# Values in one stationary operand: two products for three in a gated hybrid block

## The chip, the core and the metric

The kernel runs on one core of a Trainium2 chip. The metric is the device time of one execution in microseconds, the median over several. Five engines work side by side, each with its own queue in order: TensorE (PE, with its weight loads shown as PEld), VectorE (DVE), ScalarE (ACT), GpSimd (POOL) and SyncE (SP), which here only issues DMAs. The products go to eight banks, of 512 float32 per partition each, and ScalarE and VectorE take them from there.

## What is computed

One layer of a hybrid encoder on x of 512 positions by 1024 channels, in float32. The parts that matter here:

```
h    = rms_norm(x, g)
proj = h @ w_in          # conv B, C, in | q | k | v | forget logits | gates
F    = cumsum(log_sigmoid(f + b_f))
s    = q.k / sqrt(64) + F[t] - F[s],  s <= t
o    = softmax(s) v      # 8 heads of 64
x    = x + (sigmoid(gA) * y_conv + sigmoid(gB) * (o @ w_out_attn)) @ w_o
x    = x + w_down(silu(a) * b),  [a|b] = dwconv3(rms_norm(x) @ w_up)
out  = rms_norm(x)
```

## The kernel before

**Arithmetic.** A float32 operand is split into two parts of the type float32r: `hi`, the rounded copy (made by ScalarE), and `lo`, what is left of it (a subtraction by VectorE). A product is then three matmuls, hi by hi, lo by hi and hi by lo, which `mm3` (L240) issues one after another into the same bank. The product of the two lo parts is left out.

**Layout.** Channels or positions lie on 128 partitions. x is held as eight blocks `xs` of 128 channels by 512 positions; `xgh` and `xgl` (L384, L393) are the two parts of x times the norm's scale, which stands in `vec`, a tile with all scales and small weights as columns. Weights come in as a stream of chunks of 128 x 1024 (`raw`), and `split` (L196 to L227) makes `wh` and `wl` of each, with two buffers for each part, so that the next chunk is split while the one in use is multiplied.

**Order of the program.** (1) v and the forget logits for all positions, from eight chunks `v0` to `v7`, kb by kb (L378 to L426), while x arrives; nine calls on a tile of ones (18 PE instructions, `warm`, L101) stand ahead of them on TensorE. (2) `evac_v` (L629) scales v and splits it into `vh` and `vl`. (3) q and k of the first two pairs of heads. (4) The attention loop (L681): 32 units of (pair, head e of the pair, block qb of 128 queries). Unit i issues its two score matmuls, then one half of a projection from the list `fill` (24 matmuls, for the convolution, q, k and gates), then the transposes `tp` of unit i - 3 into one of two banks (5 and 6, in turn), and after every second query block of head 1 `attend` (L575), five units behind the scores. (5) The gates, mix, w_o, and the channel mixer, none of which the change touches.

**attend.** For a pair of heads and half of the queries (256), o of shape 128 x 256 is collected in bank 7: the first 64 partitions are head 0 and the others head 1. The stationary operand holds 64 columns of v and 64 columns of zeros, in this order for head 0 and the other way round for head 1. To this end `vh` and `vl` have three slots of 64 with zeros in the middle (two GpSimd memsets, L340). For each head and each block kb of keys three matmuls: `vh` by `pth`, `vl` by `pth`, `vh` by `ptl`, where `pth` and `ptl` are the two parts of the transposed probabilities. The last kb covers only 128 of the 256 queries. The halves have 2 and 4 blocks of keys, so an attend has 12 or 24 matmuls. Then ScalarE copies o to `oth` (L589) and VectorE makes `otl` (L590), which `ya` (L729 to L733) reads in the mix.

**The start.** L353 to L366 write out the order of the first transfers. SP's queue: first half of xs block 0, second part of chunk v0, second half of block 0, block 1, v1, block 2, v2, and so on. ScalarE's queue: first part of v0, then 40 columns of `vec` (the scales). The first `xgh` piece (L384) waits for the half of block 0 and for these columns. The rest of `vec` follows later (L366).

**What sets the order.** `keep` fixes TensorE's matmuls, the DMAs and the start in program order; ScalarE's and VectorE's other instructions are put in order by the scheduler.

Of the kernel before, what the change touches and what calls it, by code (L numbers as in the profile page):

```python
# [8 lines left out]
F32 = mybir.dt.float32  # L9
F32R = mybir.dt.float32r  # L10
AF = mybir.ActivationFunctionType
ALU = mybir.AluOpType

P = 128
D = 1024
S = 512
KB = D // P
NT = S // P
H = 8
HD = 64  # L20
# [11 lines left out]
PADL, PADR = 16, 120  # L32


G1, G2, GF, BG, CM, CF, BF = 0, 8, 16, 24, 40, 52, 184
ME, MO = 185, 186
NV = 187
VW = 4 * HD + H
PADW = {"h": 32, "l": 16}

# [17 lines left out]
def block_kernel(ctx, tc, xT, vecs, wv, win, wmix, wo, wup, wst, wdp, outT):  # L58
# [3 lines left out]
    nc = tc.nc  # L62
# [6 lines left out]
    def keep(ins):  # L69
        return tc.keep_in_program_order(ins)  # L70
# [13 lines left out]

    vec = cp.tile([P, NV], F32, tag="vec", name="vec")

    def col(i):
        return vec[:, i : i + 1]
# [221 lines left out]
    xgh = abp.tile([P, KB, S], F32R, tag="xgh", name="xgh")  # L310
    xgl = abp.tile([P, KB, S], F32R, tag="xgl", name="xgl")
    oth = abp.tile([P, 4, S], F32R, tag="oth", name="oth")
    otl = abp.tile([P, 4, S], F32R, tag="otl", name="otl")
# [20 lines left out]
    )  # L334


    vh = ap.tile([P, NT, 4, 3, HD], F32R, tag="vh", name="vh")
    vl = ap.tile([P, NT, 4, 3, HD], F32R, tag="vl", name="vl")
    for t in (vh, vl):
        nc.gpsimd.memset(t.bitcast(F32)[:, :, :, 1, :], 0.0)  # L340

    ssq = ct("ssq1")
    pa = [bank(t, f"pa{t}") for t in range(NT)]
# [4 lines left out]
    def load_x(kb, cs=slice(0, S)):  # L348
        if kb == len(xs):
            if kb % 2 == 0:  # L350
                load_x.t = ap.tile([P, 2, S], F32, tag="qt" if kb < 4 else "ka", name=f"xs{kb}", bufs=2)
            xs.append(load_x.t[:, kb % 2, :])
        keep(nc.sync.dma_start(xs[kb][:, cs], xT[:, kb, cs]))  # L353


    halves = [slice(0, S // 2), slice(S // 2, S)]
    load_x(0, halves[0])
    load(0)
    keep(nc.scalar.dma_start(vec[:, :CM], vecs[:, :CM]))
    load_x(0, halves[1])  # L360
    for kb in range(1, AHEAD + 1):
        load_x(kb)
# [2 lines left out]
        load_x(kb)  # L365
    keep(nc.sync.dma_start(vec[:, CM:], vecs[:, CM:]))  # L366

    def square_x(kb):
        if kb == 0:
            keep(nc.scalar.activation(ssq, xs[kb], AF.Square))  # L370
            return
        sq = ap.tile([P, S], F32, tag="pp", name=f"sq{kb}", bufs=NPP)
        keep(nc.scalar.activation(sq, xs[kb], AF.Square))
        keep(nc.vector.tensor_add(ssq, ssq, sq))
# [1 line left out]

    squares = ((), (0,), (1,), (2, 3), (4, 5), (6,), (7,), ())
    for kb in range(KB):  # L378
        x = xs[kb]
        cuts = halves if kb == 0 else [slice(0, S)]  # L380

        def x_hi():
            for cs in cuts:
                keep(nc.scalar.activation(xgh[:, kb, cs], x[:, cs], AF.Copy, scale=col(G1 + kb)))  # L384


        if kb == 1:
            x_hi()
        wh, wl = chunk(f"v{kb}")
        if kb != 1:  # L390
            x_hi()
        for cs in cuts:
            keep(nc.vector.scalar_tensor_tensor(  # L393
                xgl[:, kb, cs], x[:, cs], col(G1 + kb), xgh.bitcast(F32)[:, kb, cs],
                op0=ALU.mult, op1=ALU.subtract,
            ))
        for i in squares[kb]:
            square_x(i)

        def vmm(t, x, w, start, stop, parts=(0, 1)):  # L400
            xt = x[:, kb, t * P : (t + 1) * P]
            if 0 in parts:
                keep(nc.tensor.matmul(pa[t][:, :VW], xt, w[:, :VW], start=start, stop=stop))
            if 1 in parts:
                keep(nc.tensor.matmul(
                    pb[t], xt, w[:, VW:], start=start and t % 2 == 0, stop=stop and t % 2 == 1
                ))

        trio = ((xgh, wh), (xgh, wl), (xgl, wh))
        if kb == 0:  # L410

            for i, (x, w) in enumerate(trio):
                for t0 in (0, 2):
                    for part in (0, 1):
                        for t in (t0, t0 + 1):
                            vmm(t, x, w, i == 0, False, (part,))
        elif kb < KB - 1:
            for x, w in trio:
                for t in range(NT):
                    vmm(t, x, w, False, False)  # L420
        else:
            for t in range(NT):
                for i, (x, w) in enumerate(trio):
                    vmm(t, x, w, False, i == 2)
                if t == 0:
                    rc1 = rstd_col([ssq], NT, 6, "n1")  # L426
# [148 lines left out]
    def attend(pr, half):  # L575
        o = bank(7, f"o{pr}{half}")
        nk = 2 * half + 2
        for e in range(2):
            th, tl = PT.pop((pr, e, half))
            for kb in range(nk):  # L580
                cs = slice(P, 2 * P) if kb == nk - 1 else slice(0, 2 * P)
                wh = vh[:, kb, pr, e : e + 2, :].rearrange("p a b -> p (a b)")
                wl = vl[:, kb, pr, e : e + 2, :].rearrange("p a b -> p (a b)")
                mm3(
                    o[:, cs], wh, wl, th[:, kb, cs], tl[:, kb, cs],
                    e == 0 and kb == 0, e == 1 and kb == nk - 1,
                )
        hs = slice(half * 2 * P, (half + 1) * 2 * P)
        nc.scalar.activation(oth[:, pr, hs], o[:, : 2 * P], AF.Copy)  # L589
        nc.vector.tensor_sub(otl[:, pr, hs], o[:, : 2 * P], oth.bitcast(F32)[:, pr, hs])  # L590


    def run_all(fs):
# [35 lines left out]
    def evac_v(g, t):  # L629
        p = (pa, pb)[g][t]  # L630
        src = p[:, : 4 * HD].rearrange("p (a b c) -> p a b c", a=2, b=2)
        pr = slice(2 * g, 2 * g + 2)
        for e in range(2):
            nc.scalar.activation(vh[:, t, pr, 2 * e, :], src[:, :, e, :], AF.Copy, scale=rc1[:, t : t + 1])
            nc.vector.scalar_tensor_tensor(
                vl[:, t, pr, 2 * e, :], src[:, :, e, :], rc1[:, t : t + 1],
                vh.bitcast(F32)[:, t, pr, 2 * e, :], op0=ALU.mult, op1=ALU.subtract,
            )


# [446 lines left out]
def _layout(i):  # L1087

    import numpy as np

    i = {k: np.asarray(v) for k, v in i.items()}
    f = np.float32

    def cols(v):
        return v.reshape(-1, P).T

    def taps(w):
        return w.reshape(3, -1, P).transpose(2, 1, 0)

    def blocks(w):  # L1100

        k, n = w.shape
        return w.reshape(k // P, P, n // P, P).transpose(2, 1, 0, 3).reshape(n // P, P, k)

    x = i["x"][0]
    wi = i["w_in"][0]
    vecs = np.zeros((P, NV), f)
    vecs[:, G1 : G1 + 8] = cols(i["norm_mix_g"][0])
    vecs[:, G2 : G2 + 8] = cols(i["norm_ffn_g"][0])
    vecs[:, GF : GF + 8] = cols(i["norm_f_g"])  # L1110
    vecs[:, BG : BG + 16] = cols(i["b_gate"][0])
    vecs[:, CM : CM + 12] = taps(i["conv_mix_w"][0]).reshape(P, 12)
    cf = taps(i["conv_ffn_w"][0])
    cf = np.stack([cf[:, :NP], cf[:, NP:]], axis=2)
    vecs[:, CF : CF + 132] = cf.reshape(P, 132)
    for g, (me, mo) in enumerate(((1, 0), (0, 1), (-1, 0), (0, -1))):
        vecs[g * H : (g + 1) * H, BF] = i["b_f"][0]
        vecs[g * H : (g + 1) * H, ME] = me
        vecs[g * H : (g + 1) * H, MO] = mo

    wqk = wi[:, 3 * CW : 3 * CW + 2 * S]
    wvv = wi[:, 3 * CW + 2 * S : 3 * CW + 3 * S]
    o = 3 * CW + 3 * S
    wf = wi[:, o : o + H]
    win = np.concatenate([blocks(wi[:, : 3 * CW]), blocks(wqk), blocks(wi[:, o + H :])])
    wv = np.concatenate([wvv[:, : 4 * HD], wf, wvv[:, 4 * HD :]], axis=1).reshape(KB, P, S + H)
    wmix = np.concatenate([i["w_out_conv"][0], i["w_out_attn"][0]], axis=0)
    wup = blocks(i["w_up"][0])
    wup = np.stack([wup[:NP], wup[NP:]], axis=1).reshape(2 * NP, P, D)
    wdn = blocks(i["w_down"][0]).reshape(KB, P, NP, P)  # L1130
    wst = []
    for d in STEPS[0] + STEPS[1]:
        def pick(*which):
            return [wdn[2 * i + m, :, 2 * q + k] for i, q in d for m, k in which]

        w = pick((1, 1), (0, 0), (0, 1)) + pick((1, 0), (1, 0)) + pick((1, 1), (0, 0))
        wst.append(np.concatenate(w, axis=1))
    wst = np.stack(wst)
    wdp = np.concatenate([wdn[m, :, k] for m, k in PLAIN], axis=1)
    return {  # L1140
        "xT": x.T.reshape(KB, P, S).transpose(1, 0, 2),
        "vecs": vecs,
        "wv": wv,
        "win": win,
        "wmix": blocks(wmix),
        "wo": blocks(i["w_o"][0]),
        "wup": wup,
        "wst": wst,
        "wdp": wdp,
    }  # L1150
# [24 lines left out]
```

## Time and profile before

| | |
|---|---|
| median of 3 timed runs, us | 718.02 (717.55 to 1015.26) |
| span of the profiled execution, us | 716.9 |
| mean granted TensorE clock | 0.997 |
| DMA | 78.07 MB, mean 109 GB/s |
| first attend starts | 82.97 us |
| last attend ends | 188.87 us |
| ACT copy of o to oth | x8, 0.38 us each |
| DVE subtraction for otl | x8, 0.42 us each |

The page gives the span, from the first to the last instruction; the timed runs hold what lies around it too. A row of the timeline has start and duration in us, engine, line, operation, output and inputs, shape, count, and in brackets the idle time before it with what ended it. A row of groups ends in busy us, mean ns of one, and idle us before them. Matmuls overlap, so a row's duration is longer than the distance to the next row; the distance is the cost.

### The profile page before, as it was taken

Reading aid. Unit: us, or ns where it says so; the run is one execution under the profiler, and the core shown is the slowest. Engines: PE = TensorE matmul, PEld = TensorE weight load, DVE = VectorE, ACT = ScalarE, POOL = GpSimd, SP = SyncE. Lnnn points to the kernel's source line nnn. Section 1 sums busy time; section 2 is a strip of 40 time slices with the busy share of each in tenths; the row PEclk is TensorE's granted clock in tenths of the full one; section 3 lists DMA queues with packets and bytes.
Section 4 is the critical chain, followed back from the end, with each engine's and each line's share of the span. In section 5 each row is a group of like instructions: output and inputs, shape, how many; then the busy total and the mean of one; then the engine's idle time right before and its main releaser. Section 6 shows DMA issues by size and latency. Waiting matters only on the chain. (4 is left out here: it accounts for less than half of the span.)

```text
span 716.9 us, 14589 instructions
## 1 busy us (share of the span) xinstructions
PE 705.7 (98%) x6129; PEld 703.3 (98%) x6129; DVE 472.3 (66%) x711; ACT 317.6 (44%) x494; POOL 170.0 (24%) x188
## 2 busy tenths in 40 slices
PE   9999999999999999999999999999999999999996
PEld 9999999999999999999999999999999999999995
DVE  6677767665444444454458777789894677878963
ACT  6665545544433333333345434445433344444542
POOL 5124434222000000123311011045640111116202
PEclk9999999999999999999999999999999999999998
DMA  7513122122123333443314333357863233246313
GB/s 246 172 62 118 62 62 87 60 72 77 60 89 110 98 92 107 156 130 123 103 59 119 91 99 106 97 131 172 202 166 119 89 100 107 89 130 154 93 31 118
DMA packets 28113, 78.07 MB, mean 109 GB/s; under 512 B 3440, under 2 KB 6128, under 8 KB 28048
## 3 DMA queue, kind: packets, MB, share of 16 engines
q1 hardware_dynamic: 23296, 69.32, 31.5%
q0 software_dynamic: 3344, 6.59, 4.8%
q10 hardware_dynamic: 1408, 1.24, 0.5%
q8 instruction: 48, 0.79, 0.4%
q14 instruction: 17, 0.14, 0.1%
HBM read 74.97 MB, written 2.10 MB: 108 GB/s over the span
## 5 line engine op out<-in xcount | busy, mean ns | idle before, releaser
L248 PE MATMUL p_up<-x1l,wh_up 128*128 128x256 f32 x536 | 104.4, 276 | 0.0
L248 PE MATMUL p_up<-x1h,wl_up 128*128 128x256 f32 x536 | 104.4, 276 | 0.0
L248 PE MATMUL p_up<-x1h,wh_up 128*128 128x256 f32 x536 | 104.4, 276 | 0.0
L216 ACT ACTIVATE wh_up<-raw_up 128x1024 fp32r<-128x1024 f32 x44 | 46.7, 1060 | 89.1 <-PE p_up L248 68.8
L248 PEld LDWEIGHTS p_up<-x1l,wh_up 128*128 128x128 f32 x536 | 80.7, 188 | 0.0
L248 PEld LDWEIGHTS p_up<-x1h,wl_up 128*128 128x128 f32 x536 | 80.7, 188 | 0.0
L248 PEld LDWEIGHTS p_up<-x1h,wh_up 128*128 128x128 f32 x536 | 80.6, 188 | 0.0
L220 DVE TENSOR_TENSOR wl_in<-raw_in,wh_in 128x1024 fp32r<-128x1024 f32 x36 | 50.7, 1409 | 30.1 <-ACT wh_in L216 29.6
L220 DVE TENSOR_TENSOR wl_up<-raw_up,wh_up 128x1024 fp32r<-128x1024 f32 x44 | 53.8, 1223 | 20.6 <-ACT wh_up L216 20.6
L248 PE MATMUL p_in<-xgh,wh_in 128*128 128x256 f32 x288 | 56.9, 279 | 1.0 <-ACT wh_in L216 1.0
L216 ACT ACTIVATE wh_in<-raw_in 128x1024 fp32r<-128x1024 f32 x36 | 38.1, 1059 | 42.6 <-PE ya L248 12.7
L248 PE MATMUL p_in<-xgl,wh_in 128*128 128x256 f32 x288 | 56.5, 277 | 0.0
L248 PE MATMUL p_in<-xgh,wl_in 128*128 128x256 f32 x288 | 56.4, 277 | 0.0
L825 DVE TENSOR_TENSOR fz<-p_up,rb_n 128x512 f32<-128x512 f32 x44 | 30.3, 690 | 30.1 <-PE p_up L248 30.0
L838 POOL TENSOR_TENSOR ge<-fu,fu 128x512 f32<-128x512 f32 x11 | 17.1, 1551 | 126.1 <-DVE fu L498 113.3
L248 PEld LDWEIGHTS p_in<-xgh,wh_in 128*128 128x128 f32 x288 | 44.7, 188 | 1.9 <-ACT wh_in L216 1.2
L248 PEld LDWEIGHTS p_in<-xgl,wh_in 128*128 128x128 f32 x288 | 43.6, 188 | 0.0
L248 PEld LDWEIGHTS p_in<-xgh,wl_in 128*128 128x128 f32 x288 | 43.5, 188 | 0.0
L266 PE MATMUL p_up<-x1h,wh_up 128*128 128x256 f32 x168 | 40.3, 277 | 0.0
L266 PE MATMUL p_up<-x1l,wh_up 128*128 128x256 f32 x168 | 40.2, 276 | 0.0
L737 POOL TENSOR_TENSOR g<-g,g 128x512 f32<-128x512 f32 x8 | 10.3, 1292 | 121.3 <-DVE g L736 121.3
L495 DVE SCALAR_TENSOR_TENSOR fu<-fz,vec,fu 128x511 f32<-128x511 f32 x44 | 34.2, 780 | 1.5 <-ACT fu L494 1.5
(268 smaller groups left out, 2021.4 us busy)
## 6 DMA issues: line engine op xcount, KB each, us to landing
raw_up<-in_wup_dram SPq DMA_DIRECT2D x44, 512.0 KB, 3.4
raw_in<-in_win_dram SPq DMA_DIRECT2D x36, 512.0 KB, 3.5
raw_P<-in_wst_dram SPq DMA_DIRECT2D x17, 384.0 KB, 4.1
raw_F<-in_wst_dram SPq DMA_DIRECT2D x17, 256.0 KB
raw_F<-in_wst_dram POOLq DMA_DIRECT2D x17, 256.0 KB, 4.9
raw_mix<-in_wmix_dram SPq DMA_DIRECT2D x8, 512.0 KB, 3.6
raw_wo<-in_wo_dram SPq DMA_DIRECT2D x8, 512.0 KB, 6.3
xr<-in_xT_dram POOLq DMA_DIRECT2D x8, 256.0 KB, 4.9
```

The costliest lines, as they stand in the source:

```text
L216: ins = nc.scalar.activation(hi, raw, AF.Copy)
L220: ins = nc.vector.tensor_sub(lo, raw, hi.bitcast(F32))
L248: keep(nc.tensor.matmul(out[:, cs], w, x[:, cs], start=start and i == 0 and c == 0, stop=stop and i == 2 and c == len(cut) - 1,))
L266: keep(nc.tensor.matmul(out, wl if x == 1 else wh, xl if x == 2 else xh, start=opens and bk not in seen, stop=closes and bk not in left,))
L495: nc.vector.scalar_tensor_tensor(u[:, 1:], z[:, : S - 1], col(w + 1), u[:, 1:], op0=ALU.mult, op1=ALU.add)
L737: nc.gpsimd.tensor_add(a, a, b)
L825: nc.vector.tensor_mul(z, p, rb2)
L838: keep(nc.gpsimd.tensor_mul(ge, a.rearrange(halves_of, h=2), b.rearrange(halves_of, h=2)))
```

## The change

**Values.** One tile `vv` replaces `vh` and `vl`: for each block of positions and each head 128 columns, hi and lo side by side; hi in the head's own half (columns 0 to 63 for head 0, 64 to 127 for head 1), lo in the other. `evac_v` writes it with the same instructions as before. `attend` issues two matmuls in place of three, `vv` by `pth` and `vv` by `ptl`. Head 0 collects in the first 256 columns of bank 7, head 1 in the other 256. In each, the own half of the partitions holds the hi products and the other half the lo products (the lo by lo product among them). So they have to be added across partitions: ScalarE copies the other half into the own partitions of a new tile `os` (64 x 256), VectorE adds the own half, for each head; then oth and otl are made of `os`. The two memsets go.

**Start.** The first half of x's block 0 is laid on the host into `vecs`, between the scales and the rest. One DMA of 296 columns, first on SP's queue, brings both; ScalarE's queue loses its second DMA, SP's the one of the half block. The instructions that read this half read `vec`. The square of block 0 becomes two instructions of 256 columns.

```diff
+XV = 40
+NV = 187 + 256
...
-    vh = ap.tile([P, NT, 4, 3, HD], F32R, tag="vh", name="vh")
-    vl = ap.tile([P, NT, 4, 3, HD], F32R, tag="vl", name="vl")
-    for t in (vh, vl):
-        nc.gpsimd.memset(t.bitcast(F32)[:, :, :, 1, :], 0.0)
+    vv = ap.tile([P, NT, 4, 2, P], F32R, tag="vv", name="vv")
...
-    load_x(0, halves[0])
+    keep(nc.sync.dma_start(vec[:, :CM], vecs[:, :CM]))
     load(0)
-    keep(nc.scalar.dma_start(vec[:, :CM], vecs[:, :CM]))
     load_x(0, halves[1])
...
+    def x_of(kb, cs):
+        return vec[:, XV : XV + S // 2] if kb == 0 and cs.start == 0 and cs.stop == S // 2 else xs[kb][:, cs]
...
-            keep(nc.scalar.activation(ssq, xs[kb], AF.Square))
+            for h in halves:
+                keep(nc.scalar.activation(ssq[:, h], x_of(0, h), AF.Square))
...
-                wh = vh[:, kb, pr, e : e + 2, :].rearrange("p a b -> p (a b)")
-                wl = vl[:, kb, pr, e : e + 2, :].rearrange("p a b -> p (a b)")
-                mm3(
-                    o[:, cs], wh, wl, th[:, kb, cs], tl[:, kb, cs],
-                    e == 0 and kb == 0, e == 1 and kb == nk - 1,
-                )
+                os_ = slice(e * 2 * P + cs.start, e * 2 * P + cs.stop)
+                for i, x in enumerate((th, tl)):
+                    keep(nc.tensor.matmul(
+                        o[:, os_], vv[:, kb, pr, e, :], x[:, kb, cs],
+                        start=e == 0 and kb == 0 and i == 0, stop=e == 1 and kb == nk - 1 and i == 1,
+                    ))
...
-        nc.scalar.activation(oth[:, pr, hs], o[:, : 2 * P], AF.Copy)
-        nc.vector.tensor_sub(otl[:, pr, hs], o[:, : 2 * P], oth.bitcast(F32)[:, pr, hs])
+        w = ap.tile([P, 2 * P], F32, tag="os", name=f"os{pr}{half}", bufs=2)
+        for e in range(2):
+            own, other = (slice(x * HD, (x + 1) * HD) for x in (e, 1 - e))
+            oe = o[:, e * 2 * P : (e + 1) * 2 * P]
+            nc.scalar.activation(w[own, :], oe[other, :], AF.Copy)
+            nc.vector.tensor_add(w[own, :], oe[own, :], w[own, :])
+        nc.scalar.activation(oth[:, pr, hs], w, AF.Copy)
+        nc.vector.tensor_sub(otl[:, pr, hs], w, oth.bitcast(F32)[:, pr, hs])
...
+            own, other = (slice(x * HD, (x + 1) * HD) for x in (e, 1 - e))
-            nc.scalar.activation(vh[:, t, pr, 2 * e, :], src[:, :, e, :], AF.Copy, scale=rc1[:, t : t + 1])
+            nc.scalar.activation(vv[:, t, pr, e, own], src[:, :, e, :], AF.Copy, scale=rc1[:, t : t + 1])
...
+    vecs[:, XV : XV + S // 2] = x.T[:P, : S // 2]
```

How this stands in the queues. TensorE at the first attend (pair 0, first half), from its start to the first product of head 1; before:

```order
L248 MATMUL o_1176<-pth_942,vh 128x256
L248 MATMUL o_1176<-pth_942,vl 128x256
L248 MATMUL o_1176<-ptl_943,vh 128x256
L248 MATMUL o_1176<-pth_942,vh 128x128
L248 MATMUL o_1176<-pth_942,vl 128x128
L248 MATMUL o_1176<-ptl_943,vh 128x128
L248 MATMUL o_1176<-pth_982,vh 128x256 [waits Activation_49]
```

and after:

```order
L584 MATMUL o_1173<-pth_939,vv 128x256
L584 MATMUL o_1173<-ptl_940,vv 128x256
L584 MATMUL o_1173<-pth_939,vv 128x128
L584 MATMUL o_1173<-ptl_940,vv 128x128
L584 MATMUL o_1173<-pth_979,vv 128x256 [waits Activation_49]
```

Four products in place of six for a head, two of each width; the wait for the probabilities of head 1 stays.

ScalarE behind this attend (`pth` copies transposed probabilities out, `pp` is the exponential of the next scores, `wh_in` the hi part of the next weights); before:

```order
L572 ACTIVATE pth_1168<-tp_1170 128x3x128 [waits PE_49]
L589 ACTIVATE oth<-o_1176 128x256 [waits PE_49]
L549 ACTIVATE pp_1196,m_1194<-s_1191,m_1194 128x128 [waits DVE_49]
L216 ACTIVATE wh_in_1226<-raw_in_929 128x1024 [waits DMAHW6_49,PE_49,Activation_49]
L572 ACTIVATE pth_1126<-tp_1241 128x4x128 [waits PE_49]
```

and after:

```order
L572 ACTIVATE pth_1165<-tp_1167 128x3x128 [waits PE_49]
L593 ACTIVATE os_1182<-o_1173 64x256 [waits PE_49]
L549 ACTIVATE pp_1194,m_1192<-s_1189,m_1192 128x128 [waits DVE_49]
L593 ACTIVATE os_1182<-o_1173 64x256 [waits DVE_49]
L595 ACTIVATE oth<-os_1182 128x256 [waits DVE_49]
L217 ACTIVATE wh_in_1224<-raw_in_926 128x1024 [waits DMAHW5_49,PE_49,Activation_49]
L572 ACTIVATE pth_1123<-tp_1239 128x4x128 [waits PE_49]
```

Two instructions more, and the two that now stand ahead of wh_in wait for VectorE.

SP's queue at the start; before:

```order
L353 DMA xs_115<-in_xT_dram 128x256
L153 DMA raw_v_117<-in_wv_dram 128x256
L353 DMA xs_115<-in_xT_dram 128x256
L353 DMA xs_115<-in_xT_dram 128x512
L157 DMA raw_v_123<-in_wv_dram 128x520
```

and after:

```order
L355 DMA vec<-in_vecs_dram 128x296
L154 DMA raw_v_113<-in_wv_dram 128x256
L351 DMA xs_116<-in_xT_dram 128x256
L351 DMA xs_116<-in_xT_dram 128x512
L158 DMA raw_v_119<-in_wv_dram 128x520
```

Only the first transfer differs, in its source and by 40 columns.

More of the change, by code (lines that the diff above doesn't have):

```diff
@@ L32 @@
 PADL, PADR = 16, 120
-G1, G2, GF, BG, CM, CF, BF = 0, 8, 16, 24, 40, 52, 184
-ME, MO = 185, 186
-NV = 187
+G1, G2, GF, BG, CM, CF, BF = 0, 8, 16, 24, 296, 308, 440
+ME, MO = 441, 442
+XV = 40
+NV = 187 + 256
 VW = 4 * HD + H
@@ L378, in block_kernel @@
     for kb in range(KB):
-        x = xs[kb]
         cuts = halves if kb == 0 else [slice(0, S)]
@@ L383, in x_hi @@
             for cs in cuts:
-                keep(nc.scalar.activation(xgh[:, kb, cs], x[:, cs], AF.Copy, scale=col(G1 + kb)))
+                keep(nc.scalar.activation(xgh[:, kb, cs], x_of(kb, cs), AF.Copy, scale=col(G1 + kb)))
         if kb == 1:
@@ L393, in block_kernel @@
             keep(nc.vector.scalar_tensor_tensor(
-                xgl[:, kb, cs], x[:, cs], col(G1 + kb), xgh.bitcast(F32)[:, kb, cs],
+                xgl[:, kb, cs], x_of(kb, cs), col(G1 + kb), xgh.bitcast(F32)[:, kb, cs],
                 op0=ALU.mult, op1=ALU.subtract,
@@ L633, in evac_v @@
         for e in range(2):
-            nc.scalar.activation(vh[:, t, pr, 2 * e, :], src[:, :, e, :], AF.Copy, scale=rc1[:, t : t + 1])
+            own, other = (slice(x * HD, (x + 1) * HD) for x in (e, 1 - e))
+            nc.scalar.activation(vv[:, t, pr, e, own], src[:, :, e, :], AF.Copy, scale=rc1[:, t : t + 1])
             nc.vector.scalar_tensor_tensor(
-                vl[:, t, pr, 2 * e, :], src[:, :, e, :], rc1[:, t : t + 1],
-                vh.bitcast(F32)[:, t, pr, 2 * e, :], op0=ALU.mult, op1=ALU.subtract,
+                vv[:, t, pr, e, other], src[:, :, e, :], rc1[:, t : t + 1],
+                vv.bitcast(F32)[:, t, pr, e, own], op0=ALU.mult, op1=ALU.subtract,
             )
```

## The prediction

> **What bounds the kernel now.** I read the page's busy times first, then the list of waits for TensorE alone, then the stage that the change touches.
>
> ```profile
> span 716.9 us, 14589 instructions
> PE 705.7 (98%) x6129; PEld 703.3 (98%) x6129; DVE 472.3 (66%) x711; ACT 317.6 (44%) x494; POOL 170.0 (24%) x188
> ```
>
> TensorE is busy for 705.7 of 716.9 us, and the next engine, VectorE, for 66%. The waits of TensorE leave nothing in the attention stage:
>
> ```profile
> PE dn L266 <- DVE wl_F L220: 1.2, 3, 0.5
> PE p_in L248 <- ACT wh_in L216: 1.0, 1, 1.0
> ```
>
> The columns are total us, times, longest. These two rows are the longest with products of the kernel in them; dn belongs to the mixer behind attention, and the wait on wh_in comes once, ahead of the first transposes. From the first attend to the last, the stretch reads so (busy us and count of PE, PEld, DVE, ACT, POOL, then clock, DMA share, GB/s):
>
> ```profile
> 84.40:186.10 101.70, 101.70 (x872) 101.19 (x871) 63.34 (x144) 46.56 (x104) 28.75 (x41) 1.00 0.23 71
> ```
>
> TensorE is busy for all 101.70 us at the full granted clock, ScalarE for 46%, VectorE for 62%. So here time is the number of matmuls times their spacing. A matmul taken out shortens the span by its spacing, as long as no wait takes its place.
>
> **The matmuls removed.** These are the products that write o, and the two instructions that take o out:
>
> ```profile
> L248 PE MATMUL o<-pth,vh x48: 220/276/369, 83.0 to 188.6; 128*128 128x256 f32 x32, 128*128 128x128 f32 x16
> L248 PE MATMUL o<-pth,vl x48: 273/276/283, 83.2 to 188.6; 128*128 128x256 f32 x32, 128*128 128x128 f32 x16
> L248 PE MATMUL o<-ptl,vh x48: 274/276/286, 83.3 to 188.8; 128*128 128x256 f32 x32, 128*128 128x128 f32 x16
> L589 ACT ACTIVATE oth<-o x8: 372/383/384, 84.6 to 189.1; 128x256 fp32r<-128x256 f32 x8
> L590 DVE TENSOR_TENSOR otl<-o,oth x8: 415/419/420, 85.7 to 189.7; 128x256 fp32r<-128x256 f32 x8
> ```
>
> There are 144, in 8 attends; 96 stay, so 48 go: 32 with 256 moving columns and 16 with 128. The 276 ns are a latency, since they overlap. The cost is the distance from start to start (first column, us), in the first attend and at the two ends of the last:
>
> ```profile
> 82.97 0.37 PE L248 MATMUL o<-pth,vh 128*128 128x256 f32 x1
> 83.17 0.28 PE L248 MATMUL o<-pth,vl 128*128 128x256 f32 x1
> 83.29 0.28 PE L248 MATMUL o<-ptl,vh 128*128 128x256 f32 x1
> 83.40 0.22 PE L248 MATMUL o<-pth,vh 128*128 128x128 f32 x1
> 83.46 0.28 PE L248 MATMUL o<-pth,vl 128*128 128x128 f32 x1
> 83.57 0.27 PE L248 MATMUL o<-ptl,vh 128*128 128x128 f32 x1
> 83.69 0.33 PE L248 MATMUL o<-pth,vh 128*128 128x256 f32 x1
> ...
> 84.37 0.33 PE L540 MATMUL s<-a_k,a_q 128*128 128x256 f32 x1
> ...
> 186.15 0.28 PE L248 MATMUL o<-pth,vh 128*128 128x256 f32 x1
> ...
> 188.87 0.33 PE L248 MATMUL yc<-ych,wh_mix 128*128 128x256 f32 x1
> ```
>
> An attend of the first half takes 84.37 - 82.97 = 1.40 us for 12 matmuls, one of the second half 188.87 - 186.15 = 2.72 us for 24. Four of each make 4 x (1.40 + 2.72) = 16.5 us for 144, or 0.114 us each. The removed one is the middle of each trio; in the rows it takes 0.12 at 256 columns (83.17 to 83.29) and 0.11 at 128 (83.46 to 83.57), so the mean holds for it: 48 x 0.114 = **5.5 us saved**. Bounds: if a 128-column product in a pair were worth only the 0.06 that the first of a trio shows (83.40 to 83.46), it is 32 x 0.114 + 16 x 0.06 = 4.6; at most it is 48 x 0.12 = 5.8. I take 5.5, because in a pair the second 128-column product still follows the first as the middle one does now.
>
> The Trainium skill (TensorE: Matmul & The Clock Gate, section Back-to-back issue gap) gives N/2.4 + 2.5 ns for a matmul on its own, some 109 ns at 256 columns and 56 at 128. The trace agrees at 256 (0.11 to 0.12) and for the first of a 128-column trio (0.06), not for its second and third (0.11, 0.12). By that rule alone the estimate would be 32 x 0.109 + 16 x 0.056 = 4.4 us saved.
>
> **The evacuation added.** Per attend there were one ScalarE copy (0.38) and one VectorE subtraction (0.42), in series. Now there are three of each, strictly in turn: two halves of 64 partitions on each engine, then the old two on the sum. Does half the partitions halve the time? A row with 64 partitions beside one with 128:
>
> ```profile
> L482 ACT ACTIVATE a_q<-t_q 64x512 fp32r<-64x512 f32 x8 | 5.0, 631 | 3.9 <-DVE t_q L471 3.8
> L572 ACT ACTIVATE pth<-tp 128x512 fp32r<-128x512 f32 x8 | 4.7, 586 | 2.1 <-PE tp L569 2.0
> ```
>
> No: 64x512 takes 631 ns on ScalarE, 128x512 586. VectorE's pair of 64x512 further down takes 1.71, or 0.86 each. So a 64x256 piece costs 0.38 on ScalarE (the row of oth) and 0.42 on VectorE (that of otl, and half of 0.86). Per attend that is 2 x 0.38 + 2 x 0.42 = 1.6 us of chain; in all ScalarE gains 6.1 us and VectorE 6.7, which in the 96.7 us that are left of that stretch makes 54% and 72%. No engine becomes the bound.
>
> The chain can cost only through its queue: ScalarE's second os copy waits for VectorE, and the copies of tp and wh_in stand behind it. Who is late then? The transposes alternate between two banks, so the one at 94.30 needs the bank of the one at 87.44, which VectorE leaves last:
>
> ```profile
> 87.44 0.60 PE L569 MATMUL tp<-ident,pp 128*128 128x128 f32 x4
> 90.88 0.60 PE L569 MATMUL tp<-ident,pp 128*128 128x128 f32 x4
> 94.30 0.27 PE L569 MATMUL tp<-ident,pp 128*128 128x128 f32 x1
> ```
>
> ```profile
> 86.35 0.16 DVE L552 RECIPROCAL m<-m 128x1 f32<-128x1 f32 x1 [0.25 <-ACT pp L549]
> 88.32 0.43 DVE L545 CUSTOM_DVE_ANT_0 s<-s,strip 128x256 f32<-128x256 f32 x1 [1.81 <-PE s L541]
> ...
> 90.53 0.68 DVE L573 TENSOR_TENSOR ptl<-tp,pth 128x512 fp32r<-128x512 f32 x1
> ...
> 91.31 1.71 DVE L484 TENSOR_TENSOR kb<-t_k,a_k 64x512 fp32r<-64x512 f32 x2
> ```
>
> That copy ends at 91.21, 3.1 us before it is needed. The 1.6 us fit in, and VectorE sat idle for 1.81 us just where the new additions come. I cost the chain at 0; without this cover it is 1.6 us eight times, 12.8. Bounds 0 and 12.8; I take 0 because of the 3.1.
>
> After the last attend nobody hides it but yc: ya starts at 191.66 and reads the last quarter of oth and otl at 193.70, 4.8 us after o was done at 188.87.
>
> ```profile
> 191.66 0.39 PE L248 MATMUL ya<-oth,wh_mix 128*128 128x256 f32 x2
> ...
> 193.70 0.39 PE L248 MATMUL ya<-oth,wh_mix 128*128 128x256 f32 x2
> ```
>
> The chain is 3 x 0.38 + 3 x 0.42 = 2.4 us and some hand-overs. Cost 0.
>
> **The start.** One DMA less on ScalarE's queue, the same bytes; the scales now come with the first half of x, first on SP's queue and ahead of the same transfers as before.
>
> ```profile
> 1.05 4.21 PE L101 MATMUL warm<-ones 128*128 128x128 f32 x18 [1.05 <-DVE ones L93]
> 4.94 0.81 PE L403 MATMUL pa<-wh_v,xgh 128*128 128x264 f32 x2
> ...
> 8.62 0.28 PE L403 MATMUL pa<-wh_v,xgh 128*128 128x264 f32 x1
> ```
>
> ```profile
> 4.38 0.91 ACT L384 ACTIVATE xgh<-xs,vec 128x256 fp32r<-128x256 f32 x2 [2.15 <-DMA vec<-in_vecs_dram]
> 7.02 0.72 ACT L384 ACTIVATE xgh<-xs,vec 128x512 fp32r<-128x512 f32 x1 [1.74 <-DMA xs<-in_xT_dram]
> 7.81 0.64 ACT L216 ACTIVATE wh_v<-raw_v 128x520 fp32r<-128x520 f32 x1
> ```
>
> ```profile
> 0.73 0.37 SPq L353 DMA_DIRECT2D xs<-in_xT_dram  x1
> ```
>
> ```profile
> 0.00:4.94 4.94, 3.89 (x19) 3.89 (x19) 1.43 (x4) 2.05 (x4) 4.26 (x13) 1.00 0.59 135
> xs<-in_xT_dram SPq DMA_DIRECT2D x2, 128.0 KB, 2.8
> ```
>
> ScalarE waited 2.15 us for the scales. From its issue at 0.73 the first half of x takes 2.8 us, plus 20 KB at 135 GB/s, 0.15: the first xgh could begin at 3.7 instead of 4.38. But TensorE fills 1.05 to 4.94 with 18 warm products without a gap (3.89 us busy), and the first real one starts as they end, 0.1 after its xgh. So nothing is gained before 4.94. Then kb=1 starts at 8.62, after wh_v at 7.81 + 0.64 = 8.45, which follows the whole x block awaited until 7.02: a later landing would be lost one for one. The bytes ahead of it are the same; bounds -0.1 and +0.15, I take 0. The square of the first block becomes two pieces of at most 0.38 each, behind the wh_v that TensorE awaits, and two GpSimd memsets go, on an engine busy for 24%. Both 0.
>
> **Sum.** -5.5 + 0 + 0: the span goes from 716.9 to 711.4. The median run took 718.02 and the fastest 717.55, so 0.7 to 1.1 us lie around the span; I keep that distance and take 5.5 from the median 718.02: **712.5 us**. With the bounds of the removed products and of the start, and the 0.5 us between runs, the forecast's own range is 712.0 to 713.8.
>
> **The rivals.**
> 1. The hand-over blocks ScalarE (slower). Place: its second os copy, with the copy of tp and wh_in behind it. If each of VectorE's two additions stands behind a pair like the 1.71 one, the delay is 2 x 1.71 + 1.6 = 5.0 us; over the 3.1 that is 1.9 per attend, 15 in all, and 718.0 - 5.5 + 15 = 727.7. It decides from 3.1 us of delay and turns the balance at 3.1 + 0.7 = 3.8. For it: the order gives that second copy a wait on VectorE. Against: VectorE's idle 1.81 us there. A milder form, 0.2 to 0.5 us stalled per attend, gives back 1.5 to 4: 714 to 716.5.
> 2. The start gains as well: if TensorE could begin when xgh is ready, 0.7 us earlier, 711.8. For: the 2.15 us wait. Against: warm products run up to 4.94.
> 3. The pairs pay the smaller price, 4.6 saved, 713.4. For it: the 0.06 of a trio's first product. Against: the 0.11 and 0.12 of the others. By the rule of the Trainium skill above it would be 713.6.
> 4. The two products do not run at the spacing of the three, because both come right after one another from the same stationary columns; then under 2 us are saved, over 716. Nothing in the rows says so: PE and PEld have 6129 instructions each, so every product has its own load already.
>
> **How the numbers follow.** Forecast 0.70; rival 1 in full, slower than before, 0.05; its milder form 0.08; rival 2 0.07; rival 3 0.08; rival 4 0.02. The likeliest gives 712.5. The range 711.2 to 715.0 takes in rivals 2 and 3 and half of the milder form. Two per cent of the time, 14 us, is about what a measurement of this kernel can tell from no change. The saving is bounded by 5.8 + 0.8, so faster by over 2% has hardly a chance: 0.01. Slower by over 2% needs rival 1 at more than its price: 0.01. Within 2%: 0.98.
>
> **What would show it.** Right: 48 products o<-pth,vv and 48 o<-ptl,vv; the first attend from start to the next scores in about 0.92 us (8 x 0.115), the last in 1.8 (16 x 0.113); no wait of TensorE on os, oth, pth, ptl or a later wh_in; pa starting at 4.9 and kb=1 at 8.6, though the first xgh begins before 4.0. Wrong: new waits of TensorE between 80 and 190 us, an attend of over 1.0 or 2.0 us, or kb=1 more than 0.2 us off. If the span falls by more than 6.5 us, the start was worth more than I read from it.

## The result and the profile after

The changed kernel takes **712.68 us** (median of four, 712.23 to 714.26) against 718.04 for the kernel before, measured with it. The ratio of the runs is 0.9928, with a 95% interval of 0.9913 to 0.9943; one run of before, at 1015.26 us, stands far from all others and is left out of it. The profiled execution of the change took 714.26 us with this span:

```profile
span 711.7 us, 14521 instructions
PE 699.7 (98%) x6081; PEld 697.3 (98%) x6081; DVE 478.0 (67%) x727; ACT 323.7 (45%) x511; POOL 169.5 (24%) x186
```

TensorE has 48 matmuls less (6129 to 6081) and is busy for 6.0 us less; VectorE and ScalarE have 16 and 17 instructions more and 5.7 and 6.1 us more to do. The span fell by 5.2 us. In the list of TensorE's waits (total us, times, longest) the largest are

```profile
PE dn L267 <- DVE gl L872: 1.2, 1, 1.2
PE p_in L249 <- ACT wh_in L217: 1.0, 1, 1.0
...
PE pa L403 <- ACT wh_v L217: 0.7, 1, 0.7
```

No row names os, oth, pth or ptl. The wait of pa on wh_v is new and belongs to the start. The stretch from the end of the first attend to the end of the last (busy us and count of PE, PEld, DVE, ACT, POOL, clock, DMA share, GB/s) has no hole in TensorE:

```profile
84.40:184.00 99.60, 99.60 (x854) 99.09 (x852) 70.03 (x160) 53.43 (x121) 29.39 (x41) 1.00 0.25 74
```

The groups on the tiles o and os: two sets of 48 products where there were three, and ScalarE's and VectorE's pieces of 64 partitions, 0.38 and 0.42 us each:

```profile
L584 PE MATMUL o<-pth,vv x48: 220/278/369, 83.5 to 183.8; 128*128 128x256 f32 x32, 128*128 128x128 f32 x16
L584 PE MATMUL o<-ptl,vv x48: 273/279/285, 83.7 to 183.9; 128*128 128x256 f32 x32, 128*128 128x128 f32 x16
...
L593 ACT ACTIVATE os<-o x16: 376/380/384, 85.0 to 185.1; 64x256 f32<-64x256 f32 x16
L594 DVE TENSOR_TENSOR os<-o,os x16: 406/420/428, 86.2 to 185.5; 64x256 f32<-64x256 f32 x16
```

In TensorE's timeline, the first attend up to the next scores, and the two ends of the last:

```profile
83.52 0.37 PE L584 MATMUL o<-pth,vv 128*128 128x256 f32 x1
83.72 0.28 PE L584 MATMUL o<-ptl,vv 128*128 128x256 f32 x1
83.84 0.22 PE L584 MATMUL o<-pth,vv 128*128 128x128 f32 x1
83.90 0.28 PE L584 MATMUL o<-ptl,vv 128*128 128x128 f32 x1
...
84.47 0.34 PE L540 MATMUL s<-a_k,a_q 128*128 128x256 f32 x1
...
182.19 0.28 PE L584 MATMUL o<-pth,vv 128*128 128x256 f32 x1
...
184.00 0.45 PE L249 MATMUL yc<-ych,wh_mix 128*128 128x256 f32 x2
```

0.95 us for 8 products, 1.81 for 16. Four of each are 11.0 us where there were 16.5. From the first attend to the end of the last the time went from 188.87 - 82.97 = 105.90 to 184.00 - 83.52 = 100.48: 5.42 us less, which is the whole gain of the span and 0.2 more. The 0.2 are a balance: the start came 0.55 us later in this execution (83.52 for 82.97), and behind attention some 0.3 came back.

Where the start lost is in two views, ScalarE's and TensorE's:

```profile
3.04 0.51 ACT L384 ACTIVATE xgh<-vec 128x256 fp32r<-128x256 f32 x1 [0.82 <-DMA vec<-in_vecs_dram]
4.28 0.51 ACT L384 ACTIVATE xgh<-xs,vec 128x256 fp32r<-128x256 f32 x1 [0.73 <-DMA xs<-in_xT_dram]
...
8.39 0.64 ACT L217 ACTIVATE wh_v<-raw_v 128x520 fp32r<-128x520 f32 x1 [0.78 <-DMA raw_v<-in_wv_dram]
```

```profile
4.91 0.79 PE L403 MATMUL pa<-wh_v,xgh 128*128 128x264 f32 x2
...
9.07 0.39 PE L403 MATMUL pa<-wh_v,xgh 128*128 128x264 f32 x1 [0.71 <-ACT wh_v L217]
```

The first xgh begins at 3.04 where it began at 4.38, and the first product with v still at 4.91 (4.94 before). The second block of channels, kb=1, then waits for chunk v1, which landed at 8.39; before, its split began at 7.81. So kb=1 starts 0.45 us later than it did. Whether the new start does that or the landing of a transfer varies, one execution can't say. The delay is carried on one for one: from kb=1 to the first attend it is 74.44 us here and was 74.35.

### The profile page after: what moved, and what is told of

Same layout as the page of the kernel before. It is cut to its first block, busy times and chain, and to the rows that moved or that the text cites. A ratio compares the mean times of both kernels' runs of the same rounds, so it can differ in the third digit from the quotient of the medians.

```text
span 711.7 us, 14521 instructions
## 1 busy us (share of the span) xinstructions
PE 699.7 (98%) x6081; PEld 697.3 (98%) x6081; DVE 478.0 (67%) x727; ACT 323.7 (45%) x511; POOL 169.5 (24%) x186
```

## The experiments

The theory: the gain is 48 products at the spacing of the others and nothing else; the longer evacuation and the new start are both worth nothing. The rivals: the evacuation costs something that the start gives back, and the price of a product goes by its columns.

### The two parts apart, and the change again

`e1_values_only` has the values part with the start of before, `e2_start_only` the new start with the three products and the two memsets of before; the diffs are the two halves of the one shown. `e4_change_again` is the change itself, on the same chip as these.

> The values in one operand, with the start as before. Theory (the gain is the 48 products alone, the start is worth nothing): 5.5 us less than before, ratio 0.9923, and the profile shows kb=1 of the v products starting at 8.6 us as before. Rival A (the new start costs, as the one profile after has it with kb=1 at 9.07 in place of 8.62): 0.45 us faster than the whole change, 5.9 us less than before. Rival B (the new start gains): slower than the whole change by 0.5 us or more.

> The start of the change, with the values as before. Theory: no difference from before that is larger than 0.3 us, ratio 0.9996 to 1.0004. Rival A (the start costs): 0.45 us more, and kb=1 at 9.0 to 9.1 us. Rival B (the start gains): 0.5 to 0.7 us less, and kb=1 before 8.3. All expect the first xgh to begin near 3.0, and the attends to take 1.40 and 2.72 us as before.

> The change itself once more, for a second profile of its start and a timing beside the others. Theory: 5.2 to 5.6 us less than before; kb=1 lies anywhere from 8.5 to 9.1, since it follows the landing of the second chunk of v. Rival A: kb=1 at 9.0 or later again. Rival B: the span falls by over 6 us with kb=1 before 8.3.

| kernel | median, us | ratio to before (717.94), 95% | kb=1 in its profile, us |
|---|---|---|---|
| values only | 712.36 (712.12 to 713.25) | 0.9922 [0.9910, 0.9935] | 8.62 |
| start only | 718.13 (717.40 to 718.79) | 1.0003 [0.9994, 1.0012] | 8.35 |
| the change again | 712.88 (711.96 to 713.53) | 0.9925 [0.9913, 0.9938] | 8.48 |

The values are the whole gain; the start alone lies between 0.4 us faster and 0.9 us slower, which can't be told from nothing. Values only is 0.5 us under the change again, as rival A had it, and the change again gains 5.1 us where 5.2 to 5.6 were expected; both differences are inside the intervals of some 0.9 us each way. The traces are finer. From the start of the first attend to the end of the last it takes 105.9 us before and in start only, and 100.48 in the change, in values only and in the change again: 5.4 us less, and the new start changes nothing in that stretch.

The two profiles with the new start, TensorE's timeline of start only and then of the change again:

```profile
8.35 0.28 PE L406 MATMUL pa<-wh_v,xgh 128*128 128x264 f32 x1
```

```profile
8.48 0.39 PE L403 MATMUL pa<-wh_v,xgh 128*128 128x264 f32 x1
```

With the same order of transfers kb=1 came at 9.07, 8.48 and 8.35, once later and twice earlier than the 8.62 of before. Over all profiles taken, it comes at 8.53 in the mean of the seven with the new start and nine warm calls (7.93 to 9.07), and at 8.49 in the mean of the three with the old one (8.23 to 8.62). So the 0.45 us of the change's own profile lie within the scatter from one execution to another, and no cost of the new start shows.

### Two products without the new evacuation

`e3_two_products_old_copy` is the kernel before without the product of `vl` and `pth`; the lo part of v is left out of the result. Copy, subtraction and start are the old ones.

```diff
-                mm3(o[:, cs], wh, wl, th[:, kb, cs], tl[:, kb, cs], ...)
+                for i, x in enumerate((th, tl)):
+                    keep(nc.tensor.matmul(o[:, cs], wh, x[:, kb, cs], ...))
```

> The kernel before with the product of vl by pth left out, so that o lacks the lo part of v; zeros, old copy of o and old start as before. It takes the same 48 products away and adds no chain. Theory (the chain is hidden): 5.5 us less than before, the same as the values alone within 0.3 us. Rival (the chain costs something on TensorE's path): faster than the values alone by that cost, 0.2 to 0.5 us for each of 8 attends in the milder form, so 1.5 to 4 us.

Measured: 712.80 us (712.07 to 713.61), ratio 0.9928 [0.9915, 0.9942], span 710.9. The first attend takes 0.95 us, the last 1.80. With the old evacuation of two instructions it is as fast as the change with six (712.88 on the same chip); against values only (712.36) it is 0.4 us slower, a little over the 0.3 expected, where the rival had it faster. From the first attend to the end of the last it takes 100.48 us, to the hundredth what the change takes: the four instructions more per attend cost TensorE nothing there.

### How much longer the evacuation may become

Three kernels add one, two and three rounds of the hand-over to each attend, between the additions and `oth`; the one with two was added when the times of the other two were known. A round copies the 64 partitions of each head by ScalarE and takes the maximum of the copy with itself by VectorE, so the values stay what they are.

```diff
+        for r in range(R):      # R = 1, 2, 3
+            w2 = ap.tile([P, 2 * P], F32, tag="os2", ..., bufs=2)
+            for e in range(2):
+                own = slice(e * HD, (e + 1) * HD)
+                nc.scalar.activation(w2[own, :], w[own, :], AF.Copy)
+                nc.vector.tensor_tensor(w[own, :], w2[own, :], w2[own, :], op=ALU.max)
         nc.scalar.activation(oth[:, pr, hs], w, AF.Copy)
```

> The change with one more round of hand-overs in each attend: ScalarE copies both halves of os into another tile, VectorE writes them back (a maximum of the copy with itself), so the values stay. That is 2 copies and 2 VectorE instructions more, with hand-overs some 2.2 us of chain. Theory (the chain is free until the copy of tp is late; in the profile after it ends at 91.59 and the bank is needed some 2.8 us later): within 0.5 us of the change, 5 to 5.6 us less than before. Rival (the chain already stalls TensorE by small amounts, so that more of it costs in proportion): 2 us or more slower than the change.

> The change with two more rounds of the hand-over behind each attend (a round is two copies of 64 rows on ScalarE and two maxima of 64 rows on VectorE over the same rows; values unchanged), between the one more that was free and the three more that cost 7.7 us. Theory, that a chain costs nothing until it is longer than the cover of the next probabilities' bank, and that beyond it TensorE pays the remainder and a lowered clock: two more rounds add about 4 us of chain, near the edge of the cover, and the median falls between 712.7 and 715.0, with stalls of TensorE of at most 0.5 us each in the attention. Rival, that the cost grows with the number of rounds: two thirds of 7.7, so about 717.8.

> The same with three more rounds, some 6.6 us of chain in each attend. Theory: this is 3.8 us over the cover of 2.8, so TensorE waits for a copy or a subtraction of the probabilities or of weights, at most 3.8 x 8 = 30 us and at least some 4 us in all: 716 to 743 us, slower than the change, with rows of TensorE waiting on pth, ptl, tp, wh_in or wl_in between 80 and 190 us. Rival (the scheduler puts the other copies ahead of the rounds, so any length hides): within 1 us of the change.

| rounds more | median, us | before, us | ratio, 95% | TensorE waits inside attention, us |
|---|---|---|---|---|
| 1 | 712.62 (711.99 to 712.92) | 718.08 | 0.9921 [0.9907, 0.9934] | none |
| 2 | 715.00 (714.77 to 715.82) | 718.20 | 0.9958 [0.9945, 0.9970] | 1.0 |
| 3 | 720.37 (720.12 to 722.42) | 718.08 | 1.0039 [1.0026, 1.0052] | 4.7 |

One round more, 2 x 0.38 + 2 x 0.42 = 1.6 us of work eight times, is free. By the ratios the second costs 2.7 us in all (0.0037 x 718) and the third another 5.8. So the cost isn't in proportion to the rounds; it begins where a cover ends. The 715.00 lies at the very edge of what the theory gave, and the stall of 1.0 us is twice what it allowed. Set product by product beside the kernel with one round more, TensorE falls behind by 1.2 us at this stall, by 0.3 at the transposes of 138.36 and by 0.4 behind attention (p_gb, 195.87); the smaller two were not followed further. Where the stall arises wasn't foreseen either. TensorE, VectorE and ScalarE of the kernel with two rounds more:

```profile
149.78 0.36 PE L540 MATMUL s<-a_k,a_q 128*128 128x256 f32 x1
...
154.01 0.30 PE L569 MATMUL tp<-ident,pp 128*128 128x128 f32 x1 [1.00 <-DVE m L552]
```

```profile
149.00 1.43 DVE L600 TENSOR_TENSOR os<-ot 64x256 f32<-64x256 f32 x3 [0.28 <-ACT ot L599]
150.47 0.43 DVE L545 CUSTOM_DVE_ANT_0 s<-s,strip 128x256 f32<-128x256 f32 x1
...
151.10 1.23 DVE L221 TENSOR_TENSOR wl_in<-raw_in,wh_in 128x1024 fp32r<-128x1024 f32 x1
...
153.18 0.68 DVE L573 TENSOR_TENSOR ptl<-tp,pth 128x512 fp32r<-128x512 f32 x1
153.78 0.15 DVE L552 RECIPROCAL m<-m 128x1 f32<-128x1 f32 x1
```

```profile
150.01 1.06 ACT L217 ACTIVATE wh_in<-raw_in 128x1024 fp32r<-128x1024 f32 x1
150.97 0.40 ACT L601 ACTIVATE oth<-os 128x256 fp32r<-128x256 f32 x1
...
151.76 0.46 ACT L549 ACTIVATE pp<-s,m 128x256 f32<-128x256 f32 x1
```

Late is a softmax: its exponential (151.76) stands behind what the rounds pushed back on ScalarE, the reciprocal of its sum (153.78) behind wl_in, ptl and two more on VectorE, and the transposes at 154.01 need that reciprocal. It is not the copy of tp that the prediction looked at, though with three rounds both occur:

```profile
PE tp L569 <- DVE m L552: 2.2, 1, 2.2
PE tp L569 <- DVE ptl L573: 2.1, 1, 2.1
PE o L584 <- DVE ptl L573: 0.4, 1, 0.4
```

The 720.37 us lie in the theory's 716 to 743, though the wait on m, the softmax's sum, is not on its list. These 4.7 us of waits are not the whole price: from the first attend to the end of the last that kernel takes 109.2 us (83.30 to 192.52), 8.7 more than the change. Windows of 2 us behind the stall that ends at 126.03 show the rest, in the clock, the third figure from the end:

```profile
126.00:128.00 2.00, 1.97 (x12) 2.00 (x13) 1.97 (x4) 0.86 (x2) 0.45 (x1) 0.70 0.29 119
128.00:130.00 2.00, 2.00 (x11) 2.00 (x11) 1.37 (x5) 1.11 (x3) 0.67 (x2) 0.50 0.00 0
130.00:132.00 2.00, 2.00 (x18) 2.00 (x18) 1.74 (x4) 1.12 (x4) 0.30 (x1) 0.95 0.00 0
```

Products of full windows are 18 to 20; here 12 and 11. At these clocks (0.30 + 0.50 + 0.05) x 2 = 1.7 us of TensorE are lost, and behind the second stall, at 159.78, the clocks 0.73, 0.50 and 0.91 give 1.7 again. The trace's own records of the clock are sharper: 0.50 from 126.81 to 130.22 and from 160.94 to 164.35, 3.41 us each, beginning 0.8 and 1.2 us behind the end of the stall. With the stalls that makes 8.1 of the 8.7 us. Behind the 1.0 us stall of the kernel with two rounds the clock stays at 1.00. The Trainium skill (TensorE: Matmul & The Clock Gate, section What's actually happening) has the clock of an idle array halve after a window of some 3.4 us; here single stalls of 2.1 and 2.2 us were enough.

### What a product of 128 columns costs

The prediction's lower bound, and the rule that it took from the Trainium skill (TensorE: Matmul & The Clock Gate, section Back-to-back issue gap), price a product by its columns. `e9_fewer_columns` narrows 32 products of the second half's attends from 256 columns to 128; it leaves out keys 128 to 383 for the first 128 queries of that half.

```diff
-                cs = slice(P, 2 * P) if kb == nk - 1 else slice(0, 2 * P)
+                cs = slice(P, 2 * P) if kb > 0 else slice(0, 2 * P)
```

> The change with the second and third block of keys cut to 128 queries too, so 32 products of the attends of the second half have 128 columns in place of 256 (what the first 128 queries of each half take from these keys is left out). Theory (a product costs some 0.115 us whether it has 128 or 256 columns, since a trio at 128 took 0.29 and the first product behind it 0.17): the attend of 16 products still takes 1.8 us and the time is that of the change within 0.3. Rival (the cost goes by columns, 0.06 at 128): 32 x 0.055 = 1.8 us less than the change, the attend at 1.4 us.

Measured: 712.63 us (711.97 to 712.82), ratio 0.9921 [0.9907, 0.9934]: nothing gained against 712.62 for its neighbour on the chip with all columns (one round more). TensorE's timeline in its last attend:

```profile
182.26 0.28 PE L584 MATMUL o<-pth,vv 128*128 128x128 f32 x1
182.38 0.27 PE L584 MATMUL o<-ptl,vv 128*128 128x128 f32 x1
...
182.60 0.28 PE L584 MATMUL o<-ptl,vv 128*128 128x128 f32 x1
182.71 0.33 PE L584 MATMUL o<-pth,vv 128*128 128x256 f32 x1
182.88 0.28 PE L584 MATMUL o<-ptl,vv 128*128 128x256 f32 x1
```

Products of 128 columns follow each other at 0.11 us, as those of 256 do, and the whole attend takes 1.76 us where it took 1.81. From the first attend to the end of the last it is 100.24 us for 100.48: 0.24 us less, where a price by columns gives 1.8. The 0.06 from the first narrow product to the next, as at 83.84 in the change, is no price: the first wide product behind narrow ones is followed only after 0.17 (182.71 to 182.88), so what one seam gives the other takes. The theory (a price per product) holds; the rule by columns, which that section gives for a matmul on its own (56 ns at 128), is not the price of these products. Products of a single column, in plain float32, show it too, in TensorE's timeline of the change:

```profile
352.03 0.95 PE L282 MATMUL pc_n<-ones,ssq 128*128 128x1 f32 x8
352.84 0.36 PE L249 MATMUL p_up<-x1h,wh_up 128*128 128x256 f32 x1
```

Eight take 0.81 us, 0.10 each. What sets the price in place of the columns isn't shown. All these products load 128 weight columns of their own, and the loads (PEld) are busy for 99.09 of the 99.60 us of attention; but four transposes with loads of 32 columns (pz, 36.65 to 36.97 in the same trace) stand 0.11 apart as well, and no run varied the load.

### What holds the start

`e8_v1_on_act` puts the chunk that kb=1 waited for on ScalarE's queue, `e7_warm6` takes three of the nine warm calls at the start away.

```diff
+            elif k == 1:
+                keep(nc.scalar.dma_start(raw[:, :ncol], src))
```

> The change with the second chunk of v issued on ScalarE's queue behind the first, on the place that the scales have left. Theory (kb=1 starts when block 1 of x or chunk 1 of v has landed and is split, and TensorE is ready for it by 8.2 to 8.3): kb=1 starts at 8.2 to 8.5 and never waits for wh_v over 0.2 us; 0.1 to 0.6 us less than the change, if all that is ahead is carried to the end. Rival (the two queues share the same transfers' rate, so block 1 lands later in exchange): kb=1 at 8.5 to 9.1 and the time of the change.

Measured: 713.63 us (712.89 to 714.18) against 718.08, ratio 0.9933 [0.9920, 0.9947], not better than the change, and 1.0 us above its two neighbours on the chip (712.62 and 712.63). ScalarE's row and TensorE's:

```profile
6.21 0.51 ACT L386 ACTIVATE xgh<-xs,vec 128x256 fp32r<-128x256 f32 x1 [2.67 <-DMA xs<-in_xT_dram]
```

```profile
6.76 0.54 PE L405 MATMUL pa<-wh_v,xgh 128*128 128x264 f32 x2 [0.64 <-ACT xgh L386]
...
9.30 0.28 PE L405 MATMUL pa<-wh_v,xgh 128*128 128x264 f32 x1
```

The second half of block 0, which was split from 4.28 on, is now split from 6.21 on; TensorE waits for it, and kb=1 starts at 9.30, later than both the theory (8.2 to 8.5) and the rival (8.5 to 9.1) had it. In the other profiles with the new start this split begins between 4.11 and 5.29, so the transfer issued earlier on another queue seems to have taken its time from the one ahead; one execution shows it.

```diff
-NWARM = 9
+NWARM = 6
```

> The change with six warm products in place of nine at the start. Theory: what the start waits for is the second block of x and the second chunk of v, not the warm products; the first product with v then starts about 1.4 us earlier (near 3.5 us where it was 4.91), the first product of the second block still falls between 7.9 and 9.1 us, and the median stays within 1 us of the change's 712.7. Rival, that the warm products hold the start and hid a gain of the earlier transfer: the second block starts near 7.2 us and the median comes to about 711.3.

Measured: 712.45 us (711.97 to 713.53) against 718.20, ratio 0.9923 [0.9910, 0.9937]. TensorE's timeline:

```profile
1.05 2.93 PE L102 MATMUL warm<-ones 128*128 128x128 f32 x12 [1.05 <-DVE ones L94]
4.03 0.78 PE L403 MATMUL pa<-wh_v,xgh 128*128 128x264 f32 x2
...
8.45 0.29 PE L403 MATMUL pa<-wh_v,xgh 128*128 128x264 f32 x1
```

The first product with v does start earlier, by 0.88 us (the 1.4 of the expectation were too much), and kb=1 stays at 8.45, inside the spread. But it isn't a landing that holds it here: TensorE has no wait between 4.03 and 8.45. Its first 24 products with v take 4.42 us, 0.18 each, where in the change they take 3.3, 0.14 each (4.91 to 7.97, and 0.24 for the last two), because they keep a spacing of over 0.2 us until about 7 instead of until about 5.5. In this execution the gain of starting early is spent on slow products.

## Why the prediction held, and where it didn't

- **TensorE is the bound**: right. It is busy for all 99.60 us from the end of the first attend to the end of the last, and the experiments that add work to other engines are free until TensorE stalls.
- **48 products at 0.114**: right. 16.5 - 11.0 = 5.5 us in the attends, 0.115 for each product that stays; an attend of the first half takes 0.95 for the 0.92 forecast, one of the second 1.81 for 1.8. Values only and the two-product kernel with the old copy give 5.6 and 5.1 us in the median, and 5.4 both in the attention of their traces. The lower bound of 4.6, from 0.06 for a narrow product, was no bound: the narrow products alone show 0.11.
- **The evacuation at 0**: the cost is right (100.48 us of attention with the long evacuation and with the old one), its working was too short. The two engines' rows at the first attend, ScalarE then VectorE:

```profile
84.98 0.38 ACT L593 ACTIVATE os<-o 64x256 f32<-64x256 f32 x1
86.41 0.37 ACT L549 ACTIVATE pp<-s,m 128x128 f32<-128x128 f32 x1 [1.05 <-DVE m L545]
...
87.77 0.42 ACT L595 ACTIVATE oth<-os 128x256 fp32r<-128x256 f32 x1 [0.49 <-DVE os L594]
```

```profile
87.31 0.43 DVE L594 TENSOR_TENSOR os<-o,os 64x256 f32<-64x256 f32 x1 [0.24 <-ACT os L593]
88.22 0.43 DVE L596 TENSOR_TENSOR otl<-os,oth 128x256 fp32r<-128x256 f32 x1 [0.48 <-ACT oth L595]
90.91 0.68 DVE L573 TENSOR_TENSOR ptl<-tp,pth 128x512 fp32r<-128x512 f32 x1
```

  The chain ends at 88.65, 4.2 us behind the scores that follow the attend (84.47); before it ended at 86.1, 1.7 behind them (84.37). That is 2.4 us longer where the sum of durations gave 1.6: it left out an exponential that stands in between and hand-overs of 0.24 to 0.49 us. Still the copy of tp ends at 91.59, only 0.38 later than before, and its bank is next needed 2.8 us after that, in TensorE's row

```profile
94.35 0.27 PE L569 MATMUL tp<-ident,pp 128*128 128x128 f32 x1
```

  So little of the delay reaches it. That other instructions fill the chain's waits is what the rows suggest; it was not tried apart.
- **Rival 1**: its kind of loss exists, at a larger delay than "from 3.1 us", and through more than the place named. One more round, 1.6 us of work on top of the chain, still costs nothing; at two, the softmax behind the rounds is late, and at three the copy of tp as well.
- **The seam to ya at 0**: right. ya starts at 186.78, and the list of waits has no row for it.
- **The start at 0**: right for the time (1.0003), wrong for the landmark. The text called kb=1 more than 0.2 us off a sign of error; in the change's profile it is 0.45 off. The step that failed is the bound of -0.1 to +0.15, drawn from one execution. The first xgh began at 3.04 where the sum gave 3.7, and with the new start kb=1 lies between 7.93 and 9.07 in the profiles of the kernels that share its transfers and warm calls. Rival 2, a gain of the earlier scales, is refuted by start only, and with fewer warm products too.
- **Rivals 3 and 4**: rival 3 fell with the price by columns, rival 4 with the 0.115.

Two smaller slips: 36 and not all 48 of the removed products lie in the stretch that the text shortened to 96.7 us, so 97.7 are left (84.47 to 182.19); and a measurement of this kernel tells much less than 14 us from no change, some 1 us by the intervals above.

Why the early spacing of TensorE's products ends at a different moment from run to run can be read from the traces' records of the clock. The first change to full clock is recorded at 5.63 us in the change, at 6.52 before and at 7.19 with six warm calls, and between 3.92 and 7.19 in all twelve profiles; the spacing falls from 0.22 to 0.12 at that moment (5.49 to 5.80 in the change, 6.41 to 6.70 before, 7.09 to 7.26 with six). The clock column says 1.00 ahead of it only because no change is recorded there. In the kernel with three rounds more, products of 256 columns under the recorded 0.50 stand at the same 0.21 to 0.22 (127.13 to 127.56 for two), so the early products look like products at half clock. The Trainium skill (TensorE: Matmul & The Clock Gate, section What's actually happening) puts such a change down to a free-running window, whose phase varies. The records agree: in that kernel the changes lie at 3.92, 126.81, 130.22, 160.94 and 164.35, which are 36, 1, 9 and 1 times 3.41 us apart.

The new start can be left out: values only is as fast as the change.

## What to carry to other kernels

Where TensorE is busy throughout a stage at full clock, price a removed matmul by the distance between starts over a whole group, not by its columns and not by one neighbouring pair. Work added to other engines is free as long as what TensorE reads next isn't late; find that by following each tile TensorE needs next (here a copy out of a bank and a softmax's reciprocal), and leave a margin, since here a stall of 2 us cost nearly as much again in the clock. A landmark that depends on landings needs more than one profile before a bound of 0.15 us is put around it.

## What was not expected of the hardware

- A product of 128 columns with a weight load of 128 columns costs as much as one of 256: 0.11 us.
- Stalls of 2.1 and 2.2 us were each followed by 3.41 us at half the clock, which lost 1.7 us each; one of 1.0 us was not. The changes of the clock lie on a grid of 3.41 us.
- As the prediction had it from other shapes, an instruction of 64 partitions by 256 takes as long as one of 128 by 256: 0.38 us on ScalarE, 0.42 on VectorE.
- The same order of transfers landed over 1.1 us apart in the start of two executions: the split of chunk v1 began at 7.24 in the kernel with one round more, and in the change the chunk landed only at 8.39. kb=1 moved with it, from 7.93 to 9.07.
